# Norms of the token tiles: the first half's square sum as the root's bias, and a Newton step of two tensor-scalar operations

## The chip, the core and the metric

The kernel runs on one core of one Trainium2 chip. A core has five engines that work side by side and meet by semaphores: TensorE (PE, the matrix multiplier, with PEld for its weight loads), VectorE (DVE), ScalarE (ACT), GpSimd (POOL) and SyncE (SP, which here issues the DMAs). The metric is the time of one execution on the device, in microseconds; the lower the better.

## What is computed

The reference is a small encoder of two layers on 1024 tokens of width 1024, in float32. Layer 0 mixes the tokens by multi-scale pooling, layer 1 by differential attention; each is followed by a gated MLP with a short convolution. Every sub-layer starts with a root-mean-square norm over the 1024 numbers of a token, and one more norm ends the trunk:

```python
def _rms_norm(x, gain, eps=NORM_EPS):
    xf = x.astype(jnp.float32)
    y = xf * lax.rsqrt(jnp.mean(xf * xf, axis=-1, keepdims=True) + eps)
    return (y * gain.astype(jnp.float32)).astype(x.dtype)

for i in range(DEPTH):                       # DEPTH = 2
    hn = _rms_norm(h, mix_norm[i])
    y = _pool_mixer(...) if i == 0 else _diff_attention(...)
    h = h + y
    h = h + _conv_ffn(_rms_norm(h, ffn_norm[i]), ...)
return _rms_norm(h, final_norm)
```

The case is about how the one number per token, 1 / sqrt(mean + eps), is made.

## The kernel before

The 1024 tokens are eight tiles of 128 tokens, one token in each of the 128 partitions, so a norm of a tile is 128 numbers, one in each partition. Matrix products are done in float32 by splitting each operand into a high and a low part (names ending in _hi and _lo) and adding three products; the MLP's products follow a Strassen-like scheme with seven block products, whose weights are combined and split by POOL, DVE and ACT while PE works.

The helper `rstd` (line 179) makes the norm's factor from a sum of squares. ACT takes the square root of sum / 1024 + eps, with eps as a bias tile (line 190), and DVE inverts it (line 192). As that root is an approximation, a Newton step follows: with y the reciprocal and v the mean square plus eps (line 191), r = y (1.5 - 0.5 v y y) (lines 194, 196, 198: rs_p, rs_q, rs_r). Where the square sum comes in two halves, an addition (line 188) stands ahead of all that. `rstd` is called in four places:

- line 785, in `pool_prep`: eight tiles at the very start, one sum each. The input tile is squared (ACT, line 784; for two tiles DVE, line 782), and the result scales the tile into a high part (line 786, ACT) and a low part (line 787, DVE), which are named hnT_hi and hnT_lo for the first four tiles and xs_hi and xs_lo for the others. PE's pooling products (line 828, written to pl) read both. Next to that POOL scales the pooling weights (lines 799 and 802, two instructions each) and makes their low parts pw_lo (line 136), which the products pp (line 848) read.
- line 289, in `norm_to_x`: eight tiles of layer 0 and eight of layer 1, before the MLP, with two half sums each. `add_halves` (line 171) adds the sub-layer's output to each half of the tile on DVE (line 175) and squares it on ACT (line 176), one half after the other. The factor scales the tile on ACT (line 292, xs), PE transposes it (line 299, tp), DVE and ACT apply the gain (lines 309 and 331), and block combinations and their splits follow on DVE, ACT and POOL (lines 304, 305 and 340 to 344).
- line 704, at the end of each layer's last MLP product: four tiles one after another, each with two half sums of which the first has been there for long. Here the sums are a slice of three dimensions of a larger tile, with one tile in the middle dimension.
- line 628, in `tails`: the other four tiles of each layer, all four in one call, beside PE's work.

The order of the instructions on each engine is made by a list scheduler, which goes by priority and by simulated times; `rstd` stands under a raised priority (line 180). Exceptions are attention on PE, the MLP's units from the second on and the MLP's last product, where the order of the program is kept (lines 314, 722 and 727). The calls at lines 785 and 289 are in the scheduled part, those at 628 and 704 in the part in program order. The small tiles of the norm rotate through four buffers of each name.

Of the kernel before, what the change touches and what calls it, by code (L numbers as in the profile page):

```python
# [11 lines left out]
F32 = mybir.dt.float32  # L12
F32R = mybir.dt.float32r
I32 = mybir.dt.int32
AF = mybir.ActivationFunctionType
ALU = mybir.AluOpType
# [4 lines left out]
P = 128  # L21
S = 1024
D = 1024
# [17 lines left out]
NORM_EPS = 1e-6  # L41
# [48 lines left out]
def trunk_kernel(  # L90
# [24 lines left out]
    V, A, PE = nc.vector, nc.scalar, nc.tensor  # L115

    def pool(es, name, bufs=1, space=None, side=None):
        kw = {}
        if space is not None:
            kw["space"] = space  # L120
        if side is not None:
            kw["side"] = side
        if space is not DRAM:
            kw["reuse_waits"] = "tile"
        return es.enter_context(tc.tile_pool(name=name, bufs=bufs, **kw))
# [16 lines left out]
    small = pool(ctx, "small", bufs=4)  # L142
# [36 lines left out]
    def rstd(ss):  # L179
        with tc.high_priority(offset=150):  # L180
            if len(ss.shape) == 3:
                n, s0, s1 = ss.shape[1], ss[:, :, 0], ss[:, :, 1]
            else:
                n, s0, s1 = 1, ss[:, 0:1], ss[:, 1:2] if ss.shape[1] == 2 else None
            w, sfx = [P, n], "" if n == 1 else str(n)
            v = small.tile(w, F32, name="ms" + sfx)
            if s1 is not None:
                V.tensor_tensor(s0, s0, s1, ALU.add)
            y = small.tile(w, F32, name="rt" + sfx)
            A.activation(y, s0, AF.Sqrt, bias=eps, scale=1.0 / D)  # L190
            V.tensor_scalar(v, s0, 1.0 / D, NORM_EPS, ALU.mult, ALU.add)
            V.reciprocal(y, y)
            a = small.tile(w, F32, name="rs_p" + sfx)
            V.tensor_tensor(a, y, v, ALU.mult)
            b = small.tile(w, F32, name="rs_q" + sfx)
            V.scalar_tensor_tensor(b, a, -0.5, y, ALU.mult, ALU.mult)
            r = small.tile(w, F32, name="rs_r" + sfx)
            V.scalar_tensor_tensor(r, b, 1.5, y, ALU.add, ALU.mult)
            return r
# [87 lines left out]
    def norm_to_x(layer, tt, ar, h_t, ss):  # L287
        x, G = ar.x, nc.gpsimd
        r = rstd(ss)
        with tc.high_priority(offset=20 if layer else 0):  # L290
            xs = ar.tile("gc", [P, D], F32, "xs")
# [71 lines left out]
    def ffn(layer, ar, tail, extra=None):  # L363
# [263 lines left out]
        def tails():  # L627
            r = rstd(sq[0])
            yield
            yield  # L630
            prev = None
            for tt in range(4):
                tl = tail(tt, r[:, tt:tt + 1])
                next(tl, None)
                if prev is None:
                    yield
                yield
                yield
                next(tl, None)
                yield  # L640
                for _ in tl:
                    pass
                prev = tl
            yield

        def down_all():
# [50 lines left out]
            for t in range(4):  # L697
                for s in (len(steps) - 2, len(steps) - 1):
                    mms(s, t, False, s == len(steps) - 1)
                evict(3, t)  # L700
                finished(*squares.pop())
                if t:
                    next(ends[t - 1], None)
                ends.append(tail(t + 4, rstd(sq[1][:, t:t + 1])))
                if t > 1:
                    for _ in ends[t - 2]:
                        pass
# [35 lines left out]
    eps = cp.tile([P, 1], F32, name="eps")  # L743
# [570 lines left out]
    with tc.manual_schedule(engines={mybir.EngineType.PE}):  # L1314
        for g in range(H * NT + 2):
            j, i = divmod(g, NT)
# [131 lines left out]
```

## Time and profile before

| | |
|---|---|
| median of 3 runs | 2084.54 us (2083.7 to 2086.34) |
| profiled execution, its own time | 2089.84 us |
| its span, first to last instruction | 2088.0 us |
| mean granted clock of PE | 0.983 |
| median of one: rs_p, rs_q, rs_r | 0.16 us each |
| longest of one: rs_p, rs_q, rs_r | 1.85, 2.28, 1.27 us |
| longest reciprocal of the norms | 0.18 us |

How to read the profile. The page gives, for each engine, its busy time, its share of the span and its instructions; then the chain of work that ended last, followed back from the last instruction, with the share of each engine. The timeline lists instructions in order of their start: start, duration, engine, line, operation, the tile written, the tiles read, their shapes, how many were merged into the row, and in square brackets how long the engine had been idle before and what ended that. In the table by stretch of time each row has the window, its length, the busy time and the count of instructions of each engine that worked in it (PE, PEld, DVE, ACT, POOL, in this order, or only the one asked for), the granted clock of PE, the mean share of the DMA engines and GB/s. In the list of waits a row names who waited, for whom, the total in microseconds, how many times and the longest. A row of one tile's or line's instructions has the shortest, median and longest duration in nanoseconds, and the first and last start. A wait for several semaphores is put down to the one that came last.

### The profile page before, as it was taken

The numbers are of one execution on the slowest core, as the hardware profiler recorded it, in microseconds if no ns is written. First come the engines' busy times: TensorE is split into PE (matmuls) and PEld (weight loads), VectorE is DVE, ScalarE is ACT, GpSimd is POOL, SyncE is SP. The second block draws the span as 40 slices with busy tenths as digits, with TensorE's granted clock in tenths as the row PEclk, the third lists the DMA queues.
The fourth block names the chain that finished last, engine by engine and source line by source line (L and its number), as shares of the span: only waits on it lengthen the run. The fifth ranks groups of instructions, "written<-read, shape, count | busy, mean of one in ns | idle before, by whom it ended". The sixth has DMA issues, their size and how long they took to land.

```text
span 2088.0 us, 27647 instructions
## 1 busy us (share of the span) xinstructions
PE 2003.6 (96%) x9659; PEld 1665.6 (80%) x9659; DVE 1560.6 (75%) x2294; ACT 1024.4 (49%) x1838; POOL 895.3 (43%) x676
## 2 busy tenths in 40 slices
PE   5789999999999999999999998997999999999998
PEld 5768888888888877888888887875888888888886
DVE  6877777777665748899899888778667777775665
ACT  5743333333443645676667666456433333334443
POOL 4489999997000000101110110114999999930000
PEclk7889999999999999999999999999999999999999
DMA  4226445454876512122212115253345545458663
GB/s 153 99 70 198 141 154 184 132 177 151 334 239 221 207 56 66 48 75 61 61 46 77 54 35 197 101 172 118 121 160 167 172 149 179 142 191 334 201 211 132
DMA packets 221720, 301.90 MB, mean 145 GB/s; under 512 B 17852, under 2 KB 142092, under 8 KB 218764
## 3 DMA queue, kind: packets, MB, share of 16 engines
q1 hardware_dynamic: 221580, 300.13, 44.0%
q8 instruction: 76, 1.25, 0.2%
q14 instruction: 64, 0.52, 0.1%
HBM read 196.78 MB, written 90.70 MB: 138 GB/s over the span
## 4 chain that ended last, share of the span: by engine, by line
PE 59%; DVE 5%; ACT 2%; DMA 2%; issue 1%; SPq 1%; POOL 0%; ACTq 0%; DVEq 0%; POOLq 0%
PE dn L596 14%; PE up_b L422 8%; PE pj L1027 7%; PE up_c L422 5%; PE up_a L422 5%; PE sc L1113 5%; PE pj L1069 4%; PE po L1155 3%; PE aT L1144 3%; PE pj L1251 2%; DVE nm L1115 1%; DMA kf<-t 1%; ACT prob L1118 1%; DMA raw<-in_ffn_w_up_dram 0%; PE wo_acc L1251 0%
## 5 line engine op out<-in xcount | busy, mean ns | idle before, releaser
L1095 POOL TENSOR_TENSOR q_lo<-qt,q_hi 128x256 fp32r<-128x256 f32 x64 | 49.6, 776 | 683.4 <-ACT q_hi L1094 351.0
L380 POOL TENSOR_TENSOR w_lo<-s,w_hi 128x512 fp32r<-128x512 f32 x168 | 273.9, 1630 | 17.7 <-ACT w_hi L379 17.2
L596 PE MATMUL dn<-hnT_hi 128*128 128x512 f32 x560 | 218.3, 390 | 0.4 <-DVE hda L617 0.2
L596 PE MATMUL dn<-hnT_lo,hnT_hi 128*128 128x512 f32 x560 | 217.9, 389 | 0.0
L596 PE MATMUL dn<-hnT_hi,hnT_lo 128*128 128x512 f32 x560 | 217.9, 389 | 0.0
L422 PE MATMUL up_b<-x_hi,w_hi 128*128 128x512 f32 x528 | 207.2, 392 | 5.8 <-ACT x_hi L304 4.6
L422 PE MATMUL up_b<-x_lo,w_hi 128*128 128x512 f32 x528 | 206.4, 391 | 2.3 <-DVE x_lo L305 2.3
L380 POOL TENSOR_TENSOR w_lo<-raw,w_hi 128x512 fp32r<-128x512 f32 x130 | 195.1, 1501 | 30.0 <-ACT w_hi L379 26.5
L422 PE MATMUL up_b<-x_hi,w_lo 128*128 128x512 f32 x528 | 206.2, 391 | 0.0
L379 ACT CAST w_hi<-s 128x512 fp32r<-128x512 f32 x176 | 108.4, 616 | 179.1 <-PE up_b L422 87.3
L1115 DVE TENSOR_REDUCE nm<-sc 128x1 f32<-128x1024 f32 x128 | 155.8, 1217 | 15.7 <-PE sc L1113 15.0
L579 ACT CAST hnT_hi<-mst 128x1024 fp32r<-128x1024 f32 (+1 forms) x76 | 74.7, 983 | 164.7 <-PE dn L596 123.1
L1118 ACT ACTIVATE prob<-sc,nm 128x1024 f32<-128x1024 f32 x128 | 142.7, 1115 | 23.3 <-DVE nm L1115 11.6
L580 DVE TENSOR_TENSOR hnT_lo<-mst,hnT_hi 128x1024 fp32r<-128x1024 f32 (+1 forms) x76 | 86.5, 1138 | 90.1 <-ACT hnT_hi L579 90.1
L422 PE MATMUL up_a<-hnT_hi,w_hi 128*128 128x512 f32 x352 | 139.3, 396 | 1.4 <-ACT g L499 0.9
L422 PE MATMUL up_a<-hnT_lo,w_hi 128*128 128x512 f32 x352 | 138.8, 394 | 0.1
L422 PE MATMUL up_a<-hnT_hi,w_lo 128*128 128x512 f32 x352 | 138.5, 394 | 0.0
L394 POOL TENSOR_TENSOR s<-raw 128x512 f32<-128x512 f32 x84 | 133.1, 1584 | 10.3 <-DMA raw<-in_ffn_w_up_dram 4.1
L422 PE MATMUL up_c<-hnT_hi,w_lo 128*128 128x512 f32 x352 | 137.1, 389 | 0.3 <-DVE w_lo L380 0.3
L422 PE MATMUL up_c<-hnT_hi,w_hi 128*128 128x512 f32 x352 | 136.9, 389 | 0.0
L422 PE MATMUL up_c<-hnT_lo,w_hi 128*128 128x512 f32 x352 | 136.9, 389 | 0.0
L596 PEld LDWEIGHTS dn<-hnT_hi 128*128 128x128 f32 x560 | 105.1, 188 | 22.9 <-DVE hda L617 1.2
(304 smaller groups left out, 5433.3 us busy)
## 6 DMA issues: line engine op xcount, KB each, us to landing
raw<-in_ffn_w_up_dram SPq DMA_DIRECT2D x88, 512.0 KB, 4.3
mst<-m_dram SPq DMA_DIRECT2D x70, 512.0 KB, 6.2
wd<-in_ffn_w_down_dram SPq DMA_DIRECT2D x22, 1024.0 KB, 6.0
wd_dram<-wd SPq DMA_DIRECT2D x22, 1024.0 KB, 6.4
m_dram<-cm SPq DMA_DIRECT2D x80, 256.0 KB, 5.6
wst<-wd_dram SPq DMA_DIRECT2D x40, 512.0 KB, 4.8
m_dram<-gc SPq DMA_DIRECT2D x66, 256.0 KB, 6.3
wst<-in_ffn_w_down_dram SPq DMA_DIRECT2D x30, 512.0 KB, 7.2
```

The lines of the kernel that those rows point to most:

```text
L379: A.copy(hi, src)
L380: eng.tensor_tensor(lo, src, f32(hi), ALU.subtract)
L394: eng.tensor_tensor(t, a, b, op)
L422: PE.matmul(acc, l[a][:, k], r[b][:, k], start=first and n == 0, stop=n == 11, skip_group_check=True)
L579: A.copy(h_, x)
L580: V.tensor_tensor(l_, x, f32(h_), ALU.subtract)
L596: PE.matmul(banks[t], l[:, q, cols], r[:, q], start=first and cnt == 0, stop=stop and cnt == 3 * n - 1, skip_group_check=True)
L1027: PE.matmul(acc, l[:, k % 2, h], r[:, k], start=(n == 0), stop=(n == 3 * NK - 1))
L1069: PE.matmul(acc, l[:, k % 4], r[:, k], start=(n == 0), stop=(n == 3 * NK - 1))
L1113: PE.matmul(sc[:, ns_], l[:, c], ks[:, c, ns_], start=(l is qhi), stop=(l is qlo))
L1115: V.tensor_reduce(nm, sc, AX.X, ALU.max, negate=True)
L1118: A.activation(soft[j, i][c], sc, AF.Exp, bias=nm, accum_out=sm[:, c, i:i + 1])
```

## The change

For a norm of one tile, `rstd` gets a form of its own. It has no addition of the halves. With two half sums s0 and s1, DVE makes two numbers per partition from s0 alone: b0 = s0 / 1024 + eps and c0 = -0.5 b0. ACT's root then takes s1 / 1024 with b0 as its bias; with one sum it takes that sum with eps as bias, as before. v is now -0.5 times the mean square plus eps, s1 times -0.5 / 1024 plus c0 (a number per partition, or a constant where there is one sum). After the reciprocal y, written over the root, two tensor-scalar operations make the result: v times y times y, and then (v + 1.5) times y. In both y is a factor per partition, read as a scalar operand, and the only tensor input is v, which is overwritten. The norms of four tiles keep the old form.

```diff
-            w, sfx = [P, n], "" if n == 1 else str(n)
+            if n == 1:
+                v, y = (small.tile([P, 1], F32, name="rn_" + i) for i in "vy")
+                b0, c0, last = eps, -0.5 * NORM_EPS, s0
+                if s1 is not None:
+                    b0, c0 = (small.tile([P, 1], F32, name="rn_" + i) for i in "bc")
+                    V.tensor_scalar(b0, s0, 1.0 / D, NORM_EPS, ALU.mult, ALU.add)
+                    V.tensor_scalar(c0, s0, -0.5 / D, -0.5 * NORM_EPS, ALU.mult, ALU.add)
+                    last = s1
+                A.activation(y, last, AF.Sqrt, bias=b0, scale=1.0 / D)
+                V.tensor_scalar(v, last, -0.5 / D, c0, ALU.mult, ALU.add)
+                V.reciprocal(y, y)
+                V.tensor_scalar(v, v, y, y, ALU.mult, ALU.mult)
+                V.tensor_scalar(v, v, 1.5, y, ALU.add, ALU.mult)
+                return v
+            w, sfx = [P, n], str(n)
             v = small.tile(w, F32, name="ms" + sfx)
             if s1 is not None:
                 V.tensor_tensor(s0, s0, s1, ALU.add)
```

## The prediction

> **What bounds the kernel now.** I read the page first, then a table of busy time by stage, then the queues of VectorE (DVE) and GpSimd (POOL) at the places where TensorE (PE) stops.
>
> ```profile
> span 2088.0 us, 27647 instructions
> ...
> PE 2003.6 (96%) x9659; PEld 1665.6 (80%) x9659; DVE 1560.6 (75%) x2294; ACT 1024.4 (49%) x1838; POOL 895.3 (43%) x676
> ...
> PE 59%; DVE 5%; ACT 2%; DMA 2%; issue 1%; SPq 1%; POOL 0%; ACTq 0%; DVEq 0%; POOLq 0%
> ```
>
> PE is busy for 96% of the span and carries most of the chain that ended last. The other 4% can be placed by stretches of time (window, its length, then busy time and count of each engine, then the granted clock):
>
> ```profile
> 0.00:50.00 50.00, 25.32 (x145) 24.45 (x146) 34.41 (x76) 29.11 (x50) 21.51 (x19) 0.76 0.44 155
> 50.00:105.00 55.00, 42.44 (x320) 39.60 (x319) 46.74 (x105) 40.48 (x90) 26.23 (x18) 0.89 0.29 99
> 105.00:160.00 55.00, 48.22 (x192) 38.30 (x193) 39.78 (x42) 23.89 (x39) 49.26 (x33) 0.89 0.29 91
> 160.00:720.00 560.00, 558.73 (x2463) 461.43 (x2462) 406.06 (x442) 226.41 (x324) 323.78 (x204) 1.00 0.58 193
> 1380.00:1480.00 100.00, 86.03 (x385) 67.73 (x386) 74.39 (x132) 60.86 (x123) 44.94 (x31) 0.95 0.37 119
> 1480.00:2076.00 596.00, 596.00 (x2631) 493.52 (x2630) 408.74 (x419) 227.32 (x318) 349.31 (x219) 1.00 0.55 183
> ```
>
> From 160 to 720 us and from 1480 us on PE has no room: 558.73 of 560 and 596.00 of 596. So a microsecond saved before 160, or between 1380 and 1480, moves the end by a microsecond if PE was waiting for it. Those stretches hold nearly all the norms of token tiles. PE's waits there, in total, times and longest (the first three rows are of 17 to 170 us, the last of 1384 to 1480 us):
>
> ```profile
> PE tp L299 <- ACT xs L292: 12.4, 3, 6.1
> PE pl L828 <- DVE hnT_lo L132: 6.6, 1, 6.6
> PE pl L828 <- DVE xs_lo L787: 5.1, 1, 5.1
> ```
>
> ```profile
> PE tp L299 <- ACT xs L292: 9.8, 4, 4.8
> ```
>
> xs is the tile scaled by the norm's result r, so 12.4 and 9.8 us are waits at whose head a norm stands. The 5.1 us is a wait for DVE, whose queue is this there:
>
> ```profile
> 17.55 2.84 DVE L787 SCALAR_TENSOR_TENSOR hnT_lo<-ha,rs_r,hnT_hi 128x1024 fp32r<-128x1024 f32 x1
> 20.31 1.85 DVE L194 TENSOR_TENSOR rs_p<-rt,ms 128x1 f32<-128x1 f32 x1
> 22.08 0.14 DVE L191 TENSOR_SCALAR ms<-ss 128x1 f32<-128x1 f32 x1
> 22.14 0.15 DVE L192 RECIPROCAL rt<-rt 128x1 f32<-128x1 f32 x1
> 22.21 2.28 DVE L196 SCALAR_TENSOR_TENSOR rs_q<-rs_p,rt 128x1 f32<-128x1 f32 x1
> 24.41 3.44 DVE L787 SCALAR_TENSOR_TENSOR xs_lo<-ha,rs_r,xs_hi 128x1024 fp32r<-128x1024 f32 x1
> ```
>
> and POOL's queue, each row a run of instructions:
>
> ```profile
> 17.30 4.84 POOL L799 TENSOR_TENSOR rawp<-rawp,gcol 128x1024 f32<-128x1024 f32 x2 [5.80 <-DMA rawp<-in_pool_w_dram]
> 22.13 4.64 POOL L802 TENSOR_TENSOR rawp<-rawp,psc 128x1024 f32<-128x1024 f32 x2
> 32.26 7.84 POOL L136 TENSOR_TENSOR pw_lo<-rawp,pw_hi 128x512 fp32r<-128x512 f32 x4 [5.50 <-ACT pw_hi L135]
> ```
>
> rs_p and rs_q work on one number per partition, yet took 1.85 and 2.28 us. rs_p ended at 22.16, where POOL's L799 pair ended (17.30 + 4.84 = 22.14); xs_lo ended at 27.85, 1.08 after the L802 pair (22.13 + 4.64 = 26.77). The same in layer 1, DVE's rows and then POOL's:
>
> ```profile
> 1443.22 0.16 DVE L192 RECIPROCAL rt<-rt 128x1 f32<-128x1 f32 x1
> 1443.42 0.94 DVE L194 TENSOR_TENSOR rs_p<-rt,ms 128x1 f32<-128x1 f32 x1
> ```
>
> ```profile
> 1443.07 1.27 POOL L305 TENSOR_TENSOR hnT_lo<-xf,hnT_hi 128x512 fp32r<-128x512 f32 x1 [1.62 <-ACT hnT_hi L304]
> ```
>
> While one POOL instruction ran (to 1444.34), the reciprocal, with one tensor input, passed in 0.16 us; rs_p, with two, waited until 1444.36. So the dear thing about the old norm is that four of its six DVE operations (the add, rs_p, rs_q, rs_r) read two tensors and stand still while POOL works.
>
> **The change, part by part.** It concerns 32 of the 34 norms: 8 at the start with one square sum, 16 before the MLPs, and 8 at the layers' ends (there the group has one tile, so n is 1). Two norms of four tiles stay as they are.
>
> *Form.* The add and rs_p go; rs_q and rs_r become tensor-scalar operations, with one tensor input and the other factor read per partition. Counts on DVE: 6 before and 6 after with two halves (b0, c0, v, reciprocal, v, v), 5 before and 4 after with one. No DMA and no PE instruction moves.
>
> *Price undisturbed.* Steps of a dependent chain and the price of a per-partition factor:
>
> ```profile
> 2082.96 0.16 DVE L194 TENSOR_TENSOR rs_p<-rt,ms 128x1 f32<-128x1 f32 x1
> 2083.15 0.16 DVE L196 SCALAR_TENSOR_TENSOR rs_q<-rs_p,rt 128x1 f32<-128x1 f32 x1
> ```
>
> ```profile
> L1126 DVE SCALAR_TENSOR_TENSOR cc<-sums,neglam,r x64: 207/220/224, 801.0 to 1362.7; 128x1 f32<-128x1 f32 x64
> ```
>
> A step is 0.19 to 0.20 us from start to start; with one per-partition factor (L1126, median 0.22 against 0.16) it is 0.06 longer. Behind the reciprocal the old chain has three steps, the new one two with three factors: 0.20 saved, 0.18 paid. I count this as nothing; if the second factor of one instruction is free, each chain gains 0.06 more, and no row shows which. b0, c0 and the first v lie beside Square and Sqrt. The add (0.20) leaves the chain where Sqrt waited for it; at the layers' ends that is the first of four tiles, twice, 0.4; with 0.1 for the rest I take **0.5** there (0 to 1).
>
> *Start.* If the new operations pass POOL as the reciprocal does, xs_lo waits for the POOL instruction that runs when DVE comes to it, the last of L799, and not for both of L802: it ends 1.08 after 22.14 rather than after 26.77, **4.6** earlier. PE's 5.1 us wait holds that. The next stop, 6.6 us, sits behind more xs_lo on DVE and shifts with it, at best to its whole length. What is late next is pw_lo, which ends at 32.26 + 7.84 = 40.10 and is used here:
>
> ```profile
> 43.60 0.56 PE L848 MATMUL pp<-pw_hi,hnT_hi 128*128 128x256 f32 x1
> ```
>
> The cover is 3.5 us, and 5.50 us of idle POOL ahead of pw_lo that can take the delay of L802 by xs_lo (1.08) and some of the shift. If pw_lo doesn't move at all, the start gives 3.5. Bounds 0 to 6.6.
>
> *Norms before the MLPs.* DVE busy on the operations of tile rt (reciprocal, rs_p, rs_q, rs_r), in the two norm phases, and undisturbed at layer 0's end:
>
> ```profile
> 46.00:101.00 55.00, 9.02 (x32) 0.93 0.31 106
> 1384.00:1446.00 62.00, 11.00 (x32) 0.93 0.41 135
> ```
>
> ```profile
> 740.00:756.00 16.00, 2.58 (x16) 1.00 0.33 132
> ```
>
> 32 undisturbed cost 2 x 2.58 = 5.16, so 3.9 and 5.8 us are waits for POOL. For tile ss (the add and ms):
>
> ```profile
> 46.00:101.00 55.00, 2.76 (x16) 0.93 0.31 106
> 1384.00:1446.00 62.00, 3.48 (x16) 0.93 0.41 135
> ```
>
> At 0.16 each, 16 cost 2.56, so 0.2 and 0.9 more. Together 4.1 and 6.7. PE waited for 3 of the 8 tiles in layer 0 and 4 of 8 in layer 1: 4.1 x 3/8 = 1.5 and 6.7 x 4/8 = 3.4. POOL's instruction still runs, and a following DVE operation with two inputs inherits the wait; I take half, **0.8** and **1.7**. Bounds: 0, and 4.1 and 6.7, both under the 12.4 and 9.8 that PE waits.
>
> *Sum.* 4.6 + 0.8 + 1.7 + 0.5 = 7.6 us. The profiled execution took 2089.84 (span 2088.0 and 1.84 around it), so it would take 2082.2; the runs' median, 5.3 lower, goes from 2084.54 to **2076.9**.
>
> A rule to weigh, in sentences of their own: the Trainium skill, SBUF — State Buffer, section "Who interferes with whom", says that a DVE instruction with two SBUF inputs contends with a GpSimd one that reads SBUF, and one with at most one input doesn't unless it is in a two-port mode. The trace agrees on the first half (rs_p 0.94 against 0.16). The same section lists tensor_scalar among the operations that can enter a two-port mode; by that, the new operations would wait like the old. ms, the tensor-scalar here, took 0.14 us at 22.08, but there stood at the seam between two POOL runs, so that row doesn't decide.
>
> **The rivals.** *The new operations wait for POOL too.* For it: no tensor-scalar of one number was caught inside a POOL instruction. Against: the reciprocal passed. Then two waits stand where rs_p and rs_q stood, the start gives nothing, and of three stretched operations one goes: a third of 0.8 + 1.7, 0.8, and 0.5 at the ends: 2083.2.
>
> *The start doesn't arrive.* The order of the queues there is the scheduler's, and with other operations it is another: xs_lo can again fall behind the L802 pair. Then 0.8 + 1.7 + 0.5 = 3.0: 2081.5.
>
> *Slower: b0 and c0 hold up DVE.* They need the first half's square sum, and have high priority. Were they queued right behind the first half's add, DVE would stand still until the sum is there:
>
> ```profile
> 45.96 0.69 DVE L175 TENSOR_TENSOR ha<-pp,ha 128x512 f32<-128x512 f32 x1 [0.66 <-PE pp L848]
> ```
>
> ```profile
> 47.22 0.19 ACT L176 ACTIVATION_READ_ACCUMULATOR pp<-ha 128x1 f32 x1
> ```
>
> From 46.65 to 47.41 is 0.76 us; the second half's add, the evictions behind it and so PE's banks wait. Over 16 tiles 12.2, less the 7.6: 2089.1. From ten tiles (7.6 / 0.76) it eats the gain. Against it: a list scheduler places what is ready, and the second add (0.69) fills most of that time.
>
> **How the numbers follow.** The forecast has 0.54, the waiting tensor-scalars 0.2, the lost start 0.14, b0 and c0 0.12. 0.2% of 2084.5 is 4.2 us, about what a measurement of this kernel can tell from no change: faster ends below 2080.4, slower starts at 2088.7. The forecast's own range is 2068 (6.6 + 3.1 + 5.4 + 1: the upper bounds, of the norms three quarters of 4.1 and four fifths of 6.7) to 2081 (the start 3.5 and nothing else); nearly all of it is faster, about 0.5, and of the others' spread I add 0.06. Faster 0.56, same 0.32, slower 0.12. The range is 2068 to 2087; it takes in the first two rivals and leaves out the third and a little below.
>
> **What the profile would show.** Right: no operation of tile rn_v over 0.3 us between 17 and 1446 us; the xs_lo at which PE waits ending near 23 and the first pp near 39 to 40; PE's waits for xs in sum well under 12.4 and 9.8; the reciprocal straight behind Sqrt with no add before it. Wrong: operations of rn_v stretched to a POOL instruction's end (first rival); short ones, but pp still at 43 (second); DVE idle with ACT's L176 as releaser for 0.7 us a tile (third).

## The result and the profile after

The kernel after took 2074.79 us (median of 5 runs, 2068.66 to 2075.5), the kernel before, run beside it, 2084.22 (5 runs, 2082.08 to 2086.34): a ratio of 0.9949, interval 0.9934 to 0.9965, or 9.4 us less. The forecast was 7.6 us less. The profiled execution took 2074.96 us with a span of 2073.2. Line numbers behind the norm are 14 higher than before.

The same stretches as before (window, its length, busy time and count of each engine, granted clock, DMA):

```profile
0.00:50.00 50.00, 31.32 (x208) 29.93 (x209) 37.34 (x89) 35.46 (x66) 23.97 (x21) 0.90 0.49 177
50.00:105.00 55.00, 38.28 (x270) 34.63 (x268) 46.74 (x95) 39.14 (x85) 28.13 (x21) 0.87 0.31 99
105.00:160.00 55.00, 53.02 (x222) 42.96 (x223) 35.90 (x38) 21.06 (x32) 52.30 (x35) 0.94 0.35 114
160.00:720.00 560.00, 559.10 (x2478) 462.67 (x2477) 407.42 (x443) 231.76 (x330) 313.32 (x198) 1.00 0.58 193
1380.00:1480.00 100.00, 89.13 (x389) 71.29 (x388) 72.15 (x122) 57.69 (x113) 61.64 (x41) 0.93 0.35 113
```

PE did 6.0 us more in the first 50 us, at a clock of 0.90 instead of 0.76, 4.2 less in the next 55, where work that was done earlier is missing, and 4.8 more from 105 to 160: 6.6 more in all. From 160 to 720 it is full, as before. PE's waits after (three rows of 17 to 170 us, the last of 1384 to 1480 us):

```profile
PE tp L313 <- ACT xs L306: 6.9, 1, 6.9
PE pl L842 <- DVE hnT_lo L132: 6.1, 1, 6.1
PE pl L842 <- DVE xs_lo L801: 1.1, 1, 1.1
```

```profile
PE tp L313 <- ACT xs L306: 6.6, 3, 3.9
```

The wait for xs_lo fell from 5.1 to 1.1, those for xs from 12.4 to 6.9 and from 9.8 to 6.6. Up to 170 us part of that came back further on: PE then waited 4.1 us for g and 3.2 instead of 1.2 for b. VectorE's queue at the place that the prediction showed, then GpSimd's:

```profile
17.50 2.83 DVE L801 SCALAR_TENSOR_TENSOR hnT_lo<-ha,rn_v,hnT_hi 128x1024 fp32r<-128x1024 f32 x1
20.26 0.26 DVE L196 TENSOR_SCALAR rn_v<-rn_v,rn_y 128x1 f32<-128x1 f32 x1
20.57 0.20 DVE L197 TENSOR_SCALAR rn_v<-rn_v,rn_y 128x1 f32<-128x1 f32 x1
20.88 2.29 DVE L801 SCALAR_TENSOR_TENSOR xs_lo<-ha,rn_v,xs_hi 128x1024 fp32r<-128x1024 f32 x1
```

```profile
16.91 5.17 POOL L813 TENSOR_TENSOR rawp<-rawp,gcol 128x1024 f32<-128x1024 f32 x2 [5.92 <-DMA rawp<-in_pool_w_dram]
22.20 6.48 POOL L816 TENSOR_TENSOR rawp<-rawp,psc 128x1024 f32<-128x1024 f32 x2
```

While the first GpSimd run was under way (16.91 to 22.08), the two new steps took 0.26 and 0.20 us and xs_lo ended at 23.17; the prediction had 23.2. Over the whole program (minimum, median, maximum in ns):

```profile
L196 DVE TENSOR_SCALAR rn_v<-rn_v,rn_y x32: 259/272/277, 7.4 to 2068.1; 128x1 f32<-128x1 f32 x32
L197 DVE TENSOR_SCALAR rn_v<-rn_v,rn_y x32: 196/214/215, 7.7 to 2068.4; 128x1 f32<-128x1 f32 x32
```

None of 64 was drawn out. The first pp came at 36.58, earlier than the 39 to 40 of the prediction. So far the mechanism went as forecast. But the two profiles lie 14.9 us apart in span and the medians only 9.4: the first profile of before lay above the usual time, and the prediction took its largest term from it.

### The profile page after: what moved, and what is told of

The parts are those of the page before. It is cut to its first block, busy times and chain, and to the rows that moved or that the text cites. A ratio compares the mean times of both kernels' runs of the same rounds, so it can differ in the third digit from the quotient of the medians.

```text
span 2073.2 us, 27646 instructions
## 1 busy us (share of the span) xinstructions
PE 1999.2 (96%) x9659; PEld 1664.9 (80%) x9659; DVE 1553.3 (75%) x2286; ACT 1023.5 (49%) x1838; POOL 891.7 (43%) x676
## 4 chain that ended last, share of the span: by engine, by line
PE 87%; DVE 6%; ACT 2%; DMA 2%; issue 1%; SPq 1%; DVEq 0%; ACTq 0%
PE dn L610 19%; PE up_b L436 17%; PE up_c L436 11%; PE up_a L436 11%; PE pj L1041 7%; PE sc L1127 5%; PE pj L1083 4%; PE po L1169 3%; PE aT L1158 3%; PE pj L1265 2%; PE pp L862 1%; DVE nm L1129 1%; PE pl L842 1%; PE wo_acc L1265 1%; DMA kf<-t 1%
## 5 line engine op out<-in xcount | busy, mean ns | idle before, releaser
L393 ACT CAST w_hi<-raw 128x512 fp32r<-128x512 f32 x132 | 81.6, 618 | 84.8 <-PE up_c L436 80.6
```

Source lines behind the costliest of these rows:

```text
L393: A.copy(hi, src)
```

## The experiments

**First theory**, the prediction's: steps with two tensor inputs stand still behind GpSimd, and most of the gain comes from the start. **Rival**: it comes from the norms before the MLPs, by a shorter chain of steps. Four kernels, timed together with before at 2083.03 (19 runs, 2079.71 to 2089.94).

*New form at the start alone* (the condition `if n == 1:` becomes `if n == 1 and s1 is None:`).

> The new form only in the eight norms at the start (one square sum each); the other norms as before. Theory (the new operations pass POOL): the start's gain alone, PE's first products of xs_lo near 23 us and the first pp near 37 us as in the changed kernel, and the time 5 to 7 us under the kernel before (2077 to 2079 beside 2084). Rival (the shorter chain and the freed add are the gain): at most 1 us, since the add doesn't occur at the start.

Measured: 2081.15, ratio 0.9985 (0.9975 to 0.9994), 1.9 us less, where the theory asked for 5 to 7.

*New form in the MLP norms alone* (`if n == 1 and s1 is not None and len(ss.shape) == 2:`).

> The new form only in the sixteen norms before the MLPs; start and layers' ends as before. Theory: the rest of the gain, 2 to 4 us under the kernel before; first pp at 43 to 44 us as before. Rival (add and chain length): nearly all of the 9 us.

Measured: 2075.81, ratio 0.9959 (0.9946 to 0.9971), 7.2 us less. The rival is right about the place, not yet about the reason: 7.2 of the gain sits there, and 1.9 + 7.2 = 9.1 make nearly the whole.

*Two steps, but with two tensor inputs:*

```diff
-V.tensor_scalar(v, v, y, y, ALU.mult, ALU.mult)
-V.tensor_scalar(v, v, 1.5, y, ALU.add, ALU.mult)
+V.scalar_tensor_tensor(v, v, y, y, ALU.mult, ALU.mult)
+V.scalar_tensor_tensor(v, v, 1.5, y, ALU.add, ALU.mult)
```

> The changed kernel with the same operations in number and dependence, but the two Newton operations read y as a second tensor (scalar-tensor-tensor: v times y per partition times y; (v + 1.5) times y). Theory: they wait for POOL again, some of them over 1 us; the start loses its gain (first pp back to 41 to 44 us), and the time is within 3 us of the kernel before. Rival (number of operations, the bias, the new order): as fast as the changed kernel, 9 us under before.

Measured: 2073.52, ratio 0.9947 (0.9935 to 0.996): as fast as the change, though its steps did stand still (L197 up to 2.26 us). As an account of the total, the first theory falls.

*New Newton step, old add:*

```diff
-b0, c0 = (small.tile([P, 1], F32, name="rn_" + i) for i in "bc")
-V.tensor_scalar(b0, s0, 1.0 / D, NORM_EPS, ALU.mult, ALU.add)
-V.tensor_scalar(c0, s0, -0.5 / D, -0.5 * NORM_EPS, ALU.mult, ALU.add)
-last = s1
+V.tensor_tensor(s0, s0, s1, ALU.add)
```

> The Newton step as in the change, but the halves are added by DVE ahead of the root as before: no b0, no c0. Theory: most of the gain stays, 7 to 9 us under the kernel before, first pp near 37 us. Rival (the bias in place of the add is what pays): 3 us or less.

Measured: 2078.12, ratio 0.9974 (0.9963 to 0.9985), 4.9 us less, between what the theory (7 to 9) and the rival (3 or less) had said.

**Where the start's gain went.** In the second and third of these kernels xs_lo was early too, with two-input steps at the start. So the order of events at 22 us had to be looked at again in before itself.

*The kernel before once more, unchanged.*

> The kernel before once more, unchanged, for a second profile. Its first profile ran 5 us above its median, and in it rs_q came to the head of VectorE's queue at 22.21, just after GpSimd's second scaling began at 22.13. In the runs with the new form only in the MLP norms, or with two-input Newton steps, the same two-input ops slipped in just ahead of GpSimd (rs_q at 22.04, GpSimd at 22.17) and the first pp came at 36.5 to 37.3 without any one-input form at the start. If that is a close race that the first profile lost by chance, this profile can show it won: xs_lo of tile 4 ends near 23.4, the first pp starts at 36 to 39 instead of 43.60, and the time is 2079 to 2083. If the order of the instructions loses the race every time, xs_lo ends near 27.9, the first pp is at 43 to 44 and the time is 2084 to 2090.

Measured: 2082.91, span 2081.1. VectorE's queue in this second profile of before, then GpSimd's, then the first pp:

```profile
22.00 0.14 DVE L196 SCALAR_TENSOR_TENSOR rs_q<-rs_p,rt 128x1 f32<-128x1 f32 x1
22.06 1.28 DVE L787 SCALAR_TENSOR_TENSOR xs_lo<-ha,rs_r,xs_hi 128x1024 fp32r<-128x1024 f32 x1
23.26 2.32 DVE L198 SCALAR_TENSOR_TENSOR rs_r<-rs_q,rt 128x1 f32<-128x1 f32 x1
```

```profile
16.71 5.22 POOL L799 TENSOR_TENSOR rawp<-rawp,gcol 128x1024 f32<-128x1024 f32 x2 [5.87 <-DMA rawp<-in_pool_w_dram]
22.10 5.76 POOL L802 TENSOR_TENSOR rawp<-rawp,psc 128x1024 f32<-128x1024 f32 x2 [0.17 <-DMA psc<-in_pool_scale_dram]
```

```profile
37.80 0.37 PE L848 MATMUL pp<-pw_hi,hnT_hi 128*128 128x256 f32 x1
```

The pool weights had come 0.59 us earlier (GpSimd at 16.71, not 17.30), its first run was over at 21.93, and it then waited for psc until 22.10. In that gap rs_q (22.00) and xs_lo (22.06) slipped through. In the first profile GpSimd went on at 22.13 without a gap and rs_q came at 22.21: 2.28 us, and 3.44 for xs_lo. With the race won, the old form has its first pp at 37.80, the new one at 36.58: the start is worth 1.2 us there, not 4.6 or more. From here on this second profile is the one to compare with. When PE's marks are reached (us, from the two traces):

| mark | before, second profile | after | difference |
|---|---|---|---|
| first pp | 37.80 | 36.58 | -1.2 |
| first tp of layer 0's tile 2 | 56.40 | 53.26 | -3.1 |
| last pp ends | 82.23 | 77.42 | -4.8 |
| first dn of layer 0 | 528.01 | 523.32 | -4.7 |
| last sc of layer 1 ends | 1351.63 | 1345.83 | -5.8 |
| first dn of layer 1 | 1863.32 | 1855.63 | -7.7 |
| span | 2081.11 | 2073.18 | -7.9 |

The largest part of it, 3.6 us, arises between the first and the last pp, that is among the norms of layer 0. The kernel with the new form at the start alone shows how. VectorE's steps for tile 2 there, GpSimd beside them, and what PE did:

```profile
50.90 0.98 DVE L208 TENSOR_TENSOR rs_p<-rt,ms 128x1 f32<-128x1 f32 x1
51.92 1.19 DVE L210 SCALAR_TENSOR_TENSOR rs_q<-rs_p,rt 128x1 f32<-128x1 f32 x1
53.15 0.16 DVE L212 SCALAR_TENSOR_TENSOR rs_r<-rs_q,rt 128x1 f32<-128x1 f32 x1
```

```profile
50.58 2.52 POOL L319 TENSOR_TENSOR hnT_lo<-xf,hnT_hi 128x512 fp32r<-128x512 f32 x2 [0.93 <-ACT hnT_hi L318]
```

```profile
54.60 1.10 PE L313 MATMUL tp<-ident,xs 128*128 128x128 f32 x8 [2.21 <-ACT xs L306]
```

```profile
52.20:55.60 3.40, 1.19 (x13) 1.05 (x11) 2.13 (x9) 1.80 (x3) 0.90 (x1) 1.00 0.91 261
55.60:62.50 6.90, 6.90 (x35) 6.90 (x35) 4.43 (x10) 4.92 (x8) 3.79 (x4) 0.51 0.25 76
62.50:80.00 17.50, 17.46 (x147) 17.25 (x148) 11.57 (x32) 10.84 (x25) 4.37 (x5) 1.00 0.15 61
```

Two steps of one number each stood still for two GpSimd instructions; PE stopped for 2.21 us; and then its clock was 0.51 for 6.9 us in which it was busy throughout, which cost another 3.4, worked out as the half of 6.9 that was lost. A stop of 2.2 us thus cost some 5.6. The marks bear that out: this kernel's first pp was 0.6 us ahead of the change's (36.00 against 36.58), its last pp ended 4.5 behind (81.97 against 77.42). In the change, steps of the same phase during a GpSimd run (VectorE, then GpSimd):

```profile
51.33 0.21 DVE L197 TENSOR_SCALAR rn_v<-rn_v,rn_y 128x1 f32<-128x1 f32 x1
```

```profile
50.79 2.53 POOL L319 TENSOR_TENSOR hnT_lo<-xf,hnT_hi 128x512 fp32r<-128x512 f32 x2 [0.65 <-ACT hnT_hi L318]
```

and from 48 to 80 us PE was busy for 31.86 of 32.00 at full clock:

```profile
48.00:80.00 32.00, 31.86 (x256) 30.45 (x254) 25.30 (x65) 26.08 (x58) 15.67 (x13) 1.00 0.33 116
```

That is the dearest such case in the profiles. From the first pp to the last, in before's second profile, in the old form with another order of instructions and in the old six steps rewritten with one tensor input (both further below), and in the change:

```profile
37.80:82.23 44.43, 42.19 (x340) 41.38 (x339) 32.56 (x83) 30.41 (x68) 15.26 (x12) 0.96 0.30 107
38.07:80.55 42.48, 40.86 (x340) 39.85 (x339) 31.89 (x83) 30.35 (x68) 15.26 (x12) 1.00 0.31 112
36.07:76.83 40.76, 40.67 (x340) 39.76 (x339) 31.76 (x85) 29.85 (x66) 15.58 (x13) 1.00 0.32 115
36.58:77.42 40.84, 40.70 (x338) 39.80 (x339) 32.16 (x85) 30.41 (x68) 16.75 (x14) 1.00 0.31 109
```

The old form took 3.6 and 1.6 us longer than the change, the first time by stops and the clock (0.96), the second by stops alone, at full clock. The six one-input steps took as long as the change.

**Second theory**: standing still costs, but in the MLP norms, where it stops PE and can pull the clock down. **Rival**: only the number of steps counts (six in before, four in the change). Timed together, before at 2082.17 (20 runs, 2079.29 to 2086.88):

*All six old steps, each with one tensor input:*

```diff
-V.tensor_tensor(s0, s0, s1, ALU.add)
+V.tensor_scalar(s1, s1, 1.0, s0, ALU.mult, ALU.add)
...
-V.tensor_tensor(a, y, v, ALU.mult)
-V.scalar_tensor_tensor(b, a, -0.5, y, ALU.mult, ALU.mult)
-V.scalar_tensor_tensor(r, b, 1.5, y, ALU.add, ALU.mult)
+V.tensor_scalar(a, y, 1.0, v, ALU.mult, ALU.mult)
+V.tensor_scalar(b, a, -0.5, y, ALU.mult, ALU.mult)
+V.tensor_scalar(r, b, 1.5, y, ALU.add, ALU.mult)
```

> The kernel before with its own algebra and all of its six steps for norms of one tile (add, mean, reciprocal, p, q, r), but each step that had two tensor inputs written as a tensor-scalar operation with a per-partition factor. Theory A (two-input steps, the add among them, stand still behind GpSimd's instructions, and that was the cost): as the change, -6 to -10 us against before. Theory B (what counts is how many steps stand one behind the other between the second half's square sum and r; six in before, four in the change): 0 to -3 us against before, since the steps are all there and each is 0.05 us longer.

Measured: 2077.25, ratio 0.9971 (0.9962 to 0.998), 4.9 us less with not a step fewer. That lies between the two forecasts, 6 to 10 and 0 to 3: the form counts by itself in this order of instructions, but is not the whole. Step p in this kernel, and in the next:

```profile
L201 DVE TENSOR_SCALAR rs_p<-rt,ms x32: 200/214/216, 7.5 to 2071.1; 128x1 f32<-128x1 f32 x32
```

```profile
L195 DVE TENSOR_TENSOR rn_p<-rn_y,rn_v x32: 144/159/1844, 7.4 to 2073.6; 128x1 f32<-128x1 f32 x32
```

*The add gone, the old Newton step kept* (the half sum enters as the bias; then p, q and r as before).

> The change with its first half only: the half sum enters the root as its bias, so that the add is gone; the Newton step stays the three old operations with two tensor inputs. With the complement (add kept, Newton step new) at -4.9 us and the whole at -9.4 us: if the add's standing still is what costs most, -7 to -9.5 us; if each step less in the chain is worth the same, about -5 us; if the Newton step's standing still is what costs most (theory A as the prediction had it), -1 to -3 us.

Measured: 2080.8, ratio 0.9991 (0.9982 to 1.0), 1.4 us less. With one step fewer, but three that can stand still, it is 3.6 us slower than the six steps that can't; the two ranges meet only at 2078.73. In this pair, then, the Newton step's standing still is what costs most.

*Three kernels in another order.* That two-input steps were as fast as the change could be luck of the order. With the norms' priority at 30 places, `tc.high_priority(offset=30)` instead of 150, the scheduler puts instructions of VectorE elsewhere: 42 to 68 of some 2290 in the traces of the three pairs, matched by line and tiles alone. Timed together, before at 2082.01 (24 runs, 2078.69 to 2087.56). The old form:

> The kernel before with the norms' priority raised by 30 places instead of 150, which moves some 190 lines of VectorE's order. One of three kernels with this other order, to see how much of a difference is the order's own. If orders differ by little, within 2 us of before. If the order alone is worth several us, it can lie 3 us or more to either side.

Measured: 2084.54 (2082.05 to 2086.7), ratio 1.0009 (1.0 to 1.0019). Two steps with two tensor inputs:

> The change with its Newton step as two operations with two tensor inputs each, in the other order (priority 30 instead of 150). In the order of 150 it was as fast as the change, although 7.9 us and 4.2 us of its steps in the MLP norms stood still behind GpSimd. Theory A (standing still costs; that order hid it by luck): 2 to 5 us slower than the change in the same other order, between it and the kernel before. Theory B (the number of steps counts, two inputs or one): within 1.5 us of the change in the same other order.

Measured: 2078.24 (2073.86 to 2079.37), ratio 0.9977 (0.9968 to 0.9986). The change:

> The change itself in the other order (priority 30 instead of 150). If its gain is its own and not that of one lucky order, 6 to 10 us faster than the kernel before in the same other order. If the gain is the order's, less than 3 us.

Measured: 2075.14 (2072.46 to 2076.51), ratio 0.9963 (0.9949 to 0.9976). Against the old form in the same order the gain is 9.4 us here as well. The two-input steps lie between: fewer steps are worth 6.3 in this order, the form another 3.1 (the ranges overlap, so that 3.1 is the less certain number). Both theories hold a part, but how much each is worth is not settled. The form gave 4.9 with six steps in the order of 150, 3.1 with four in this one and nothing with four in the order of 150. The order alone made before 2.5 us slower, and it took the kernel of two two-input steps from 9.5 us under before to 3.8. The six one-input steps were tried in one order only. Why the order of 150 hid the standing still is not settled: in that kernel layer 0's tile 6 came to tp at 81.95 and not at 88.22, so the tiles follow one another differently, and which change of order did it was not tried.

**Does a gain at the start reach the end?** *40 matmuls into the stop:*

```diff
+if hf == 0 and (g, dd) == (3, 0):
+    fill = ar.tile("ps_dn", [P, 512], F32, "fill")
+    for _ in range(40):
+        PE.matmul(fill[:, 0:256], xs_hl[4][1][:, 0:P], bands[0][:, 0:256], start=True, stop=True,
+                  skip_group_check=True)
```

> The change with 40 extra matmuls on TensorE in its stop of 6.1 us at the start (25.4 to 31.5), into a PSUM tile that nobody reads. In the change's profile the clock was at half from 26.3 to 36.5, with some 5 us of matmuls in it, so 2.5 us of TensorE's time lost. If that loss reaches the end, the first pp comes 2 to 3 us earlier (34 instead of 36.6) and the time is 1.5 to 2.5 us below the change's, 2072 to 2073.5. If VectorE's splitting of the pl tiles and GpSimd's pw_lo (done at 37.9) set the pace there, the time stays within 0.5 us of the change's.

Measured: 2075.65, ratio 0.9963 (0.9949 to 0.9977), no faster than the change. The clock was full from 23.9 on and the first pp came at 35.09, 1.5 us earlier, but the lead was 1.0 at the last pp and gone at the first up_b (106.53 against 106.58). The theory's 2 to 3 us at pp and 1.5 to 2.5 us at the end were both missed.

*Tiles 5 to 7 prepared later:*

```diff
-for tt in range(8):
+for tt in range(5):
     pool_prep(tt)
 pool_weights()
...
 pool_band(0)
+for tt in range(5, 8):
+    pool_prep(tt)
```

> The change with the preparation of tiles 5 to 7 placed behind the first band stage, which doesn't read them. In the change's profile VectorE made two xs_lo of these tiles (3.21 and 3.28 us, drawn out by GpSimd's scaling) while six finished pl tiles waited for their splitting, and TensorE stood still from 25.4 to 31.5. If the start reaches the end, TensorE's stop of 6.1 us shrinks to about 3, the first pp comes at 33 to 35 instead of 36.6 and the time is 2 to 4 us below the change's (2071 to 2073). If the stretch of layer 0's norms (VectorE over nine tenths busy from 75 to 97, first up_b at 106.5 in three kernels whose first pp lay between 35.1 and 37.3) takes the lead back, as it did with the extra matmuls, the first up_b stays at 106 to 107.5 and the time within 1 us of the change's.

Measured: 2069.17 (2065.92 to 2072.68), ratio 0.9934 (0.9918 to 0.995), 12.8 us less than before. The change timed beside it was the one with priority 30, at 2075.14, 6.0 more. The change with priority 150, from which this kernel is made, was not timed beside it. It was 9.4 less than the before timed with it, so some 3 us of the 12.8 are this edit's, and the two intervals overlap. PE's stops in it from 20 to 40 us, instead of 2.23, 1.15 and, before the seventh pl tile, 6.07 us:

```profile
23.55 0.36 PE L842 MATMUL pl<-band,hnT_hi 128*128 128x256 f32 x1 [1.50 <-DVE rn_y L195]
31.72 0.58 PE L862 MATMUL pp<-pw_lo,hnT_hi 128*128 128x256 f32 x1 [2.56 <-POOL pw_lo L136]
```

The first pp came at 27.89 and the first up_b at 103.82: of 8.7 us at pp 2.8 are left there, and 2.3 in the span of this profile, which is of the slowest of its runs. Much of the 8.7 is work put off, as the first tp shows (45.81, against 45.18 in the change). The two profiles of before, one program with the race lost and won, show it without an edit: 5.8 us apart at the first pp (43.60 and 37.80), 4.9 at the first up_b (114.57 and 109.64) and at layer 0's first dn (532.94 and 528.01), 6.9 in span. So a lead from the start can reach the end, in part or nearly whole.

## Why the prediction was right, and where it wasn't

*The form.* Right. The new steps pass GpSimd (0.20 to 0.28 us each), so the first rival is out, and the kernel with all six steps in that form shows that it is worth time by itself, in the one order that was tried. The Trainium skill, SBUF — State Buffer, section "Who interferes with whom", lists tensor_scalar among what can contend, when its operands meet the conditions of a two-port mode; for one number per partition no run here shows it.

*Undisturbed price.* Right: from the reciprocal to r's use 0.78 us before, 2075.84 to 2076.62 in the second profile, and 0.76 after, 2067.92 to 2068.68. Here are the last norm's rows after:

```profile
2067.92 0.16 DVE L195 RECIPROCAL rn_y<-rn_y 128x1 f32<-128x1 f32 x1 [0.48 <-ACT rn_y L193]
2068.12 0.27 DVE L196 TENSOR_SCALAR rn_v<-rn_v,rn_y 128x1 f32<-128x1 f32 x1
2068.43 0.21 DVE L197 TENSOR_SCALAR rn_v<-rn_v,rn_y 128x1 f32<-128x1 f32 x1
2068.68 0.75 DVE L1427 SCALAR_TENSOR_TENSOR hdb<-hdb,rn_v,gf 128x512 f32<-128x512 f32 x1
```

The second per-partition factor is not free: 0.15 us with none (b0, L190), 0.21 with one (L197) and 0.27 with two (L196).

*Start, 4.6 us.* Too large: 1.9 when it is changed alone. The failing step is that rs_q's 2.28 us was read as the rule. Where the race is lost the term is about right: the two profiles of before lie 4.9 us apart at the first up_b. But it hung on a race of about 0.1 us that one profiled execution lost and the other won; how often it is lost is not on record. That the profiled execution lay 5.3 us above the median was the warning. The later stops did shift, as forecast, but the argument that a microsecond saved before 160 us is a microsecond at the end, if PE waited for it, held only in part: the extra matmuls' 1.5 us were gone by 106.

*Norms before the MLPs, 0.8 + 1.7 us.* Too small: 7.2 when they are changed alone. The failing step is the pricing of VectorE's waits: three or four of eight tiles, and half of that, as if one of them could cost PE no more than itself. In one profile a stop of 2.21 us cost some 5.6, because of the clock, which the sum left out; in another, a stop of 1.57 us before the same tile cost no clock. And the shorter chain was priced at nothing, while in the other order two steps fewer were worth 6.3. How the 7.2 divide between these is open.

*Layers' ends, 0.5 us.* Right in size: between the second profile of before and after, the difference grows by 0.2 in layer 0's end (tp from 4.7 to 4.9) and by 0.2 in layer 1's (from its first dn to the span, 7.7 to 7.9).

*Sum.* 7.6 against 9.4 is near by luck, by two errors that cancel: 2.7 too much at the start, 4.7 too little at the MLP norms. The second rival (the start's gain lost, 3.0 left) had the start nearly right and the rest as small as the forecast. The third rival's sign was seen in layer 1 alone (VectorE's waits from 1372 to 1470 us, before's second profile and then after):

```profile
DVE ss L188 <- ACT wo_acc L176: 2.0, 2, 1.2
```

```profile
DVE rn_b L190 <- ACT wo_acc L176: 4.1, 6, 1.2
```

b0 stood at the head of the queue in six waits of 0.7 us on average, as that rival said, where the add stood in two. Layer 1's norms gained 1.9 us all the same (5.8 to 7.7 in the table). What those waits took from it was not tried.

## What to carry to other kernels

If a step of one number per partition takes over a microsecond, ask what its engine shares with another, and write it with a per-partition factor rather than a second tensor. A wait that hangs on two engines' starts within 0.1 us of each other is not yet a term of a sum: take a second profile, above all where the profiled execution is off the median. A stop of PE is priced with the clock that may drop behind it, and where the norm chain is what PE waits for, fewer steps can count. An edit also moves the scheduler's order, and that alone was worth 2.5 us and more here: test a small gain in a second order.

## What the runs showed of the clock

PE's clock goes to half and back in pieces of 3.41 us, and a full stop isn't needed. Worked out from the clock's and PE's records of all 14 profiles: of 86 full-clock pieces with a half-clock piece next, in 80 PE had been busy for less than 48% of the piece, against 10 of the 8127 that a full piece followed; and all 86 returns to full clock came after a piece in which it was busy for 85% or more. The stops of about 2.2 us before tile 2's tp show it. In the first profile of before it was spread over two pieces, and the clock stayed full; in the second it lay mostly in one, and the next ran at half (two rows of the first profile, then two of the second):

```profile
58.70:62.10 3.40, 1.95 (x18) 1.80 (x16) 3.10 (x7) 1.74 (x5) 2.52 (x2) 1.00 0.58 177
62.10:66.00 3.90, 3.13 (x27) 3.09 (x28) 2.60 (x9) 3.02 (x6) 0.00 (x0) 1.00 0.39 115
```

```profile
54.60:58.00 3.40, 1.60 (x14) 1.61 (x15) 2.13 (x11) 1.92 (x4) 0.29 (x1) 0.99 0.72 202
58.00:61.40 3.40, 3.40 (x18) 3.40 (x17) 1.47 (x5) 3.02 (x5) 1.79 (x2) 0.51 0.34 100
```

1.95 of 3.40 us busy kept the clock, 1.60 lost it. The Trainium skill, TensorE: Matmul & The Clock Gate, section "Part 1: The HAM clock gate", has the half rate follow on at least one idle window of some 3.4 us, and the windows running freely. The length and the free running agree; that the window has to be idle doesn't, and the measurement decides. So, by an estimate from these pieces, the same stop can cost 2.2 us or 4 to 6, by where it falls: one half-clock piece loses 1.7 us, two lose 3.4.
